# One issue run for each group of two-head products in a hybrid SSD, convolution and attention layer

## The chip, the cores and the metric

One Trainium2 chip, one core. The metric is device time in microseconds (us) of one execution; the median of three runs of the kernel before is 1844.33 us (1840.27 to 1845.91).

## The reference

One layer over 2048 tokens of width 1024. One input projection feeds three mixers, whose gated outputs go through one output projection, a residual and a gated side input. Two of the mixers matter here.

- SSD: 16 heads of 64 columns, chunks of 128 tokens. Per chunk and head, `y = y_diag + y_off`: `y_diag` is a masked 128x128 matrix (made from B, C and the cumulated decays) times the weighted inputs, `y_off` is the decayed C times the state that came into the chunk. The state of a chunk is `h * exp(dec) + new`, one chunk after the other.
- Sliding-window attention: 8 heads of 64, blocks of 128 queries against the block before (kk = 0) and their own block (kk = 1). Softmax weights times values gives the output: two products per block and head, summed.

All is in float32; the projections are made of three products of split halves (high and low part).

## The kernel before, in words

The tokens go in 4 chunks `c` of 512, each of 4 blocks `b` of 128. The first half of the program runs chunks 0 and 1, the second chunks 2 and 3. In each half, units run in the order C0 A0 S0 S1 C1 A1 S2 S3 G1 C2 A2 S4 S5 C3 A3 S6 S7 (line 986): C is convolution, A a pair of attention heads, S a pair of SSD heads, G a group's B and C. Each unit runs for both chunks. A unit has a front (input projections by `proj`, lines 443 to 445, 128x512 products on TensorE, and the eviction of their results) and a back, a Python generator that is put on a list and advanced by one step after every few products of the fronts that follow (`advance`, lines 215 to 218). So the small products of a back are written in between the long products of later fronts.

The framework then fixes the order on every engine when the program is built: a list scheduler with a cost model of its own gives each engine the next instruction whose inputs are made by its reckoning. On the chip every queue runs in that order, and an instruction that waits holds all behind it.

In SSD (`ssd_back`, lines 877 to 944) the back makes `xd` and `xw` (weighted inputs), `eA` and `Ab` (exponentials, from a load of `Ab`, line 868, whose slot in a ring of four 128x1024 tiles, shared with `eA` and with the attention scores, must have come free), four products into `ps_m` (line 910), then the states `H` one after the other on VectorE (line 918, two half-width instructions for each), and then for each block the diagonal products (line 937, `Ab` and `xd`) and the state products (line 940, `eA` and `hin[b]`). Each product has 64 output columns: the two heads of a pair go to partitions 0 to 63 and 64 to 127 of the one `ps_y` bank. The result is read by line 942 and stored by line 944.

In attention (`attn_back`, lines 740 to 861) the weights are transposed on TensorE and copied to `pT` (`turn`, lines 809 to 823), and `mix` (line 838) makes the products with the values, again with two heads in the two halves of `ps_y`. `mix(0)` is written ahead of `turn(1)`, `mix(1)` a step after it.

There are 32 groups of SSD products (8 pairs of heads, 4 chunks) and 16 groups of attention products (4 pairs, 4 chunks). A float32 product shows as two instructions in the trace, so a full group has 32.

Of the kernel before, what the change touches and what calls it, by code (L numbers as in the profile page):

```python
# [14 lines left out]
P = 128  # L15
# [3 lines left out]
TC = 512  # L19
NCHUNK = T // TC  # L20
NB = TC // P
# [40 lines left out]
def hybrid_block_kernel(  # L62
# [16 lines left out]
    V, A, G, PE = nc.vector, nc.scalar, nc.gpsimd, nc.tensor  # L79
# [8 lines left out]
    def ps(tag):  # L88
        return psum.tile([P, TC], F32, tag=tag, name=f"ps_{tag}", bufs=PSB[tag])
# [4 lines left out]
    def t512(name, dtype=F32):  # L94
        return wk.tile([P, TC], dtype, tag="t", name=name, bufs=10)

    def t1024(name):
        return wk.tile([P, 2 * TC], F32, tag="t4", name=name, bufs=4)
# [23 lines left out]
    def pc(name, i=0, n=1):  # L122
        o, w = _par[name]
        return par_sb[:, o + i:o + i + n]
# [221 lines left out]
    with ExitStack() as c1:  # L346
# [10 lines left out]
        hn, rows, kT, vN = {}, {}, {}, {}  # L357
# [144 lines left out]
        def transposes(src):  # L502
            pt = ps("m")
            for b in range(NB):
                PE.transpose(pt[:, b * P:(b + 1) * P], src[:, b * P:(b + 1) * P], ident)
            return pt
# [201 lines left out]
        def attn_front(j, p, c, bias, wq, wg):  # L708
            (pq,) = yield from proj([wq], c)
            qh, ql = t512("qh", F32R), t512("ql", F32R)  # L710
            A.mul(qh, pq, 0.125)
            V.scalar_tensor_tensor(out=ql, in0=pq, scalar=0.125, in1=qh.bitcast(F32), op0=ALU.mult, op1=ALU.subtract)


            qq = [qpair("qh2"), qpair("ql2")]
            for o_ in range(2):
                r = slice(64 * o_, 64 * o_ + 64)
                for t, src in zip(qq, (qh, ql)):
                    for hh in range(2):
                        nc.scalar.dma_start(out=t[r, hh, :].bitcast(F32), in_=src[64 * hh:64 * hh + 64, :].bitcast(F32))  # L720
            yield
            (pg,) = yield from proj([wg], c)
            g2 = silu2(pg, "ag2")
            pending.append(attn_back(j, c, bias, qq, g2))
            yield

        def prev(c, i):

            if c % 2 == 0:
                return kv_tail[i]  # L730
            t = kT[c - 1][i] if i < 2 else vN[c - 1]
            return t[:, TC - P:TC]
# [7 lines left out]
        def attn_back(j, c, bias, qq, g2):  # L740
# [66 lines left out]
            pTs = {}  # L807

            def turn(u):
                for bb in range(2):  # L810
                    b = 2 * u + bb
                    first = c == 0 and b == 0
                    pt = ps("m")
                    for hh in range(2):
                        for kk in range(1 if first else 0, 2):
                            PE.transpose(pt[:, (hh * 2 + kk) * P:(hh * 2 + kk + 1) * P], S[u][:, bb, hh, kk * P:(kk + 1) * P], ident)  # L816
                    pTs[b] = t512("pT")
                    if first:
                        for hh in range(2):
                            s_ = slice((hh * 2 + 1) * P, (hh * 2 + 2) * P)  # L820
                            A.copy(pTs[b][:, s_], pt[:, s_])
                    else:
                        A.copy(pTs[b], pt)

            def mix(u, po):
                for bb in range(2):
                    b = 2 * u + bb
                    first = c == 0 and b == 0
                    for kk in range(1 if first else 0, 2):
                        for hh in range(2):  # L830
                            r = slice(64 * hh, 64 * hh + 64)
                            if kk == 1:
                                vv = vN[c][:, b * P + 64 * hh:b * P + 64 * hh + 64]
                            elif b > 0:
                                vv = vN[c][:, (b - 1) * P + 64 * hh:(b - 1) * P + 64 * hh + 64]
                            else:
                                vv = prev(c, 2)[:, 64 * hh:64 * hh + 64]
                            PE.matmul(  # L838
                                po[r, b * P:(b + 1) * P],
                                lhsT=vv,  # L840
                                rhs=pTs[b][:, (hh * 2 + kk) * P:(hh * 2 + kk + 1) * P],
                                start=(kk == 0 or first),
                                stop=(kk == 1),
                            )

            yield
            scores(0)
# [4 lines left out]
            yield  # L852
            turn(0)
            yield
            po = ps("y")
            mix(0, po)
            turn(1)
            yield
            mix(1, po)
            V.tensor_tensor(out=g2, in0=po, in1=g2, op=ALU.mult)  # L860
            nc.sync.dma_start(out=y_d[12 + j, :, c * TC:(c + 1) * TC], in_=g2)

# [14 lines left out]
        def ssd_back(q, p, c, Ab, xv, z2, tiles, tabs):  # L877
            Bn, CT, CBm = tiles
            dt, acs, eat, dec = tabs
            h0 = 2 * q  # L880
            sl = slice(p * TC, (p + 1) * TC)

            def v4(t):
                return t.rearrange("p (b h d) -> p b h d", b=NB, h=2)

            def bc(t):
                return t[:, p * NB:(p + 1) * NB, h0:h0 + 2].unsqueeze(3).to_broadcast([P, NB, 2, 64])

            def h2(t):
                return t.rearrange("p (h l) -> p h l", h=2)  # L890

            pt = transposes(xv)
            xd = t512("xd")
            V.tensor_tensor(out=v4(xd), in0=v4(pt), in1=bc(dt), op=ALU.mult)
            xw = t512("xw")
            V.tensor_tensor(out=v4(xw), in0=v4(xd), in1=bc(dec), op=ALU.mult)

            eA = t1024("eA")
            A.activation(eA, Ab, AF.Exp)
            for hh in range(2):  # L900
                for b in range(NB):
                    o_ = hh * TC + b * P
                    A.activation(Ab[:, o_:o_ + P], Ab[:, o_:o_ + P], AF.Relu, scale=-1.0, bias=acs[:, p * NB + b, h0 + hh:h0 + hh + 1])  # L903
            A.activation(Ab, Ab, AF.Exp, scale=-1.0)
            yield

            pst = ps("m")
            for b in range(NB):
                bs = slice(b * P, (b + 1) * P)
                PE.matmul(pst[:, bs], lhsT=Bn[:, p * TC + b * P:p * TC + (b + 1) * P], rhs=xw[:, bs], start=True, stop=True)  # L910
            H = tp.tile([P, NB - 1, P], F32, tag="H", name="H", bufs=1)
            hin = [hcar[:, q, :]] + [H[:, b, :] for b in range(NB - 1)]

            def state(b):
                nxt = hin[b + 1] if b < NB - 1 else hcar[:, q, :]
                for hh in range(2):
                    d_ = slice(64 * hh, 64 * hh + 64)
                    V.scalar_tensor_tensor(
                        out=nxt[:, d_],
                        in0=hin[b][:, d_],  # L920
                        scalar=eat[:, p * NB + b, h0 + hh:h0 + hh + 1],
                        in1=pst[:, b * P + 64 * hh:b * P + 64 * hh + 64],
                        op0=ALU.mult,
                        op1=ALU.add,
                    )

            V.tensor_tensor(out=h2(eA), in0=h2(eA), in1=CT[:, sl].unsqueeze(1).to_broadcast([P, 2, TC]), op=ALU.mult)
            V.tensor_tensor(out=h2(Ab), in0=h2(Ab), in1=CBm[:, sl].unsqueeze(1).to_broadcast([P, 2, TC]), op=ALU.mult)
            for b in range(NB - 1):
                state(b)  # L930
            yield
            py = ps("y")
            for b in range(NB):
                bs = slice(b * P, (b + 1) * P)
                for hh in range(2):
                    r = slice(64 * hh, 64 * hh + 64)
                    PE.matmul(py[r, bs], lhsT=xd[:, b * P + 64 * hh:b * P + 64 * hh + 64], rhs=Ab[:, hh * TC + b * P:hh * TC + (b + 1) * P], start=True, stop=False)  # L937
                for hh in range(2):
                    r = slice(64 * hh, 64 * hh + 64)
                    PE.matmul(py[r, bs], lhsT=hin[b][:, 64 * hh:64 * hh + 64], rhs=eA[:, hh * TC + b * P:hh * TC + (b + 1) * P], start=False, stop=True)  # L940
            state(NB - 1)
            V.scalar_tensor_tensor(out=xv, in0=xv, scalar=pc("sd", q), in1=py, op0=ALU.mult, op1=ALU.add)
            V.tensor_tensor(out=xv, in0=xv, in1=z2, op=ALU.mult)
            nc.sync.dma_start(out=y_d[q, :, c * TC:(c + 1) * TC], in_=xv)
# [80 lines left out]
    with ExitStack() as c2:  # L1025
# [4 lines left out]
        for c in range(NCHUNK):  # L1030
# [7 lines left out]
            for n, (dp, kg) in enumerate(steps):  # L1038
# [4 lines left out]
                for kk in range(4):  # L1043
                    yh, yl = ys[4 * kg + kk]
                    first, last = kg + kk == 0, kg == 3 and kk == 3
# [159 lines left out]
```

## Time and profile before

| what | value |
|---|---|
| median of three runs | 1844.33 us |
| the profiled execution | 1850.51 us, of it 1848.7 us span |
| TensorE busy | 1810.7 us (98%) |
| VectorE busy | 1385.1 us (75%) |
| ScalarE busy | 818.6 us (44%) |
| mean granted TensorE clock | 0.994 |

TensorE instructions overlap, and the busy time counts an instruction from its start to its modelled end. What a piece of work costs on TensorE is therefore read here from start to start: from the start of the last instruction ahead of it to the start of the first behind it.

### The profile page before, as it was taken

How to read it: one execution, taken by the hardware profiler on the slowest of the kernel's cores; microseconds unless marked ns; L12 is line 12 of the kernel's file. 1: busy time of each engine (PE TensorE's matmuls, PEld its weight loads, DVE VectorE, ACT ScalarE, POOL GpSimd, SP SyncE). 2: the span in 40 equal slices, each digit the busy share in tenths (PEclk: the TensorE clock that was granted, in tenths of full speed). 3: DMA queues.
4: the chain of work that ended last, by engine and by line, in shares of the span. 5: the costliest groups of instructions: out<-in, count | busy, mean ns of one | idle time of the engine just before them, and what ended most of it. 6: DMA issues, size and time to landing. Idle time of an engine off the chain costs nothing.

```text
span 1848.7 us, 25168 instructions
## 1 busy us (share of the span) xinstructions
PE 1810.7 (98%) x9386; PEld 1461.6 (79%) x9386; DVE 1385.1 (75%) x2400; ACT 818.6 (44%) x1565; POOL 0.2 (0%) x4
## 2 busy tenths in 40 slices
PE   6999999999999999999999999999999999999998
PEld 5877787787888778878788887877888788887887
DVE  6859769759869875976975996988777867466543
ACT  5525425524726542542653371465444444343331
POOL 0000000000000000000000000000000000000000
PEclk9999999999999999999999999999999999999999
DMA  7443233224433433333332332346677766578554
GB/s 234 132 133 98 80 102 96 61 78 106 171 112 111 121 102 104 91 87 89 100 115 76 101 99 87 82 145 230 214 242 236 245 228 199 202 240 280 189 188 131
DMA packets 118982, 265.09 MB, mean 143 GB/s; under 512 B 12619, under 2 KB 20428, under 8 KB 118860
## 3 DMA queue, kind: packets, MB, share of 16 engines
q1 hardware_dynamic: 108428, 246.65, 40.9%
q10 hardware_dynamic: 10432, 16.83, 4.1%
q8 instruction: 74, 1.21, 0.3%
q14 instruction: 48, 0.39, 0.1%
HBM read 205.05 MB, written 39.50 MB: 132 GB/s over the span
## 4 chain that ended last, share of the span: by engine, by line
PE 78%; DMA 8%; DVE 6%; ACT 4%; issue 2%; ACTq 1%; SPq 0%; DVEq 0%
PE ps_pp L443 15%; PE ps_pp L444 14%; PE ps_pp L445 14%; PE ps_pp L1048 4%; PE ps_pp L1049 4%; PE ps_pp L1050 4%; PE ps_pp L208 3%; PE ps_pp L209 3%; PE ps_pp L207 3%; PE ps_m L766 2%; PE ps_y L940 2%; PE ps_y L838 2%; DMA Ab<-acs_d 2%; PE ps_y L937 2%; PE ps_m L816 1%
## 5 line engine op out<-in xcount | busy, mean ns | idle before, releaser
L443 PE MATMUL ps_pp<-al,whi 128*128 128x512 f32 x1344 | 536.6, 400 | 13.6 <-DVE al L393 10.4
L444 PE MATMUL ps_pp<-ah,wlo 128*128 128x512 f32 x1344 | 534.5, 398 | 0.0
L445 PE MATMUL ps_pp<-ah,whi 128*128 128x512 f32 x1344 | 534.1, 397 | 0.0
L191 DVE TENSOR_TENSOR wlo<-wst,whi 128x1024 fp32r<-128x1024 f32 x214 | 234.1, 1102 | 179.8 <-ACT whi L190 179.4
L443 PEld LDWEIGHTS ps_pp<-al,whi 128*128 128x128 f32 x1344 | 254.4, 189 | 73.1 <-DVE al L393 10.4
L190 ACT CAST whi<-wst 128x1024 fp32r<-128x1024 f32 x214 | 202.9, 951 | 242.0 <-DMA wst<-in_w_gate_dram 86.1
L691 DVE SCALAR_TENSOR_TENSOR acc<-gl,par_sb,acc 128x1024 f32<-128x1024 f32 x240 | 307.3, 1280 | 2.3
L444 PEld LDWEIGHTS ps_pp<-ah,wlo 128*128 128x128 f32 x1344 | 254.6, 189 | 55.8 <-issue 6.5
L445 PEld LDWEIGHTS ps_pp<-ah,whi 128*128 128x128 f32 x1344 | 254.5, 189 | 54.4 <-issue 4.9
L489 DVE SCALAR_TENSOR_TENSOR cv<-raw,par_sb,cv 128x512 f32<-128x512 f32 x144 | 107.6, 747 | 22.7 <-ACT cv L487 22.0
L208 PE MATMUL ps_pp<-ah,wlo 128*128 128x512 f32 x256 | 100.2, 391 | 3.7 <-DVE wlo L191 3.7
L1048 PE MATMUL ps_pp<-bl,whi 128*128 128x512 f32 x256 | 101.5, 399 | 0.6 <-ACT whi L190 0.6
L1048 PE MATMUL ps_pp<-al,whi 128*128 128x512 f32 x256 | 100.4, 393 | 0.7 <-DVE al L191 0.7
L1049 PE MATMUL ps_pp<-bh,wlo 128*128 128x512 f32 x256 | 101.1, 395 | 0.0
L1050 PE MATMUL ps_pp<-bh,whi 128*128 128x512 f32 x256 | 100.7, 394 | 0.0
L207 PE MATMUL ps_pp<-al,whi 128*128 128x512 f32 x256 | 100.1, 391 | 0.6 <-ACT whi L190 0.5
L1049 PE MATMUL ps_pp<-ah,wlo 128*128 128x512 f32 x256 | 100.1, 391 | 0.0
L1050 PE MATMUL ps_pp<-ah,whi 128*128 128x512 f32 x256 | 100.0, 390 | 0.0
L209 PE MATMUL ps_pp<-ah,whi 128*128 128x512 f32 x256 | 99.7, 389 | 0.0
L796 ACT ACTIVATE S<-S,nm 128x256 f32<-128x256 f32 (+1 forms) x128 | 62.8, 492 | 80.0 <-DVE nm L782 74.6
L903 ACT ACTIVATE Ab<-Ab,acs 128x128 f32<-128x128 f32 x256 | 82.4, 391 | 0.4
L937 PE MATMUL ps_y<-Ab,xd 128*64 128x128 f32 x512 | 61.5, 282 | 2.0 <-issue 2.0
(235 smaller groups left out, 2592.1 us busy)
## 6 DMA issues: line engine op xcount, KB each, us to landing
wst<-in_w_in_dram SPq DMA_DIRECT2D x88, 512.0 KB, 3.5
wst<-in_w_out_dram SPq DMA_DIRECT2D x64, 512.0 KB, 5.1
Ab<-acs_d SPq DMA_DIRECT2D x64, 256.0 KB, 4.5
ysd<-y_d SPq DMA_DIRECT2D x32, 512.0 KB, 5.5
wst<-in_w_gate_dram SPq DMA_DIRECT2D x32, 512.0 KB, 3.5
gl<-in_xT_dram SPq DMA_DIRECT2D x16, 512.0 KB, 4.0
qh<-qh ACTq DMA_DIRECT2D x64, 128.0 KB, 2.4
ql<-ql ACTq DMA_DIRECT2D x64, 128.0 KB, 2.4
```

The lines of the kernel that those rows point to most:

```text
L190: A.copy(hi, src)
L191: V.tensor_tensor(out=lo, in0=src, in1=hi.bitcast(F32), op=ALU.subtract)
L207: PE.matmul(out, lhsT=hi[:, k, :], rhs=al, start=start and k == 0, stop=False)
L208: PE.matmul(out, lhsT=lo[:, k, :], rhs=ah, start=False, stop=False)
L209: PE.matmul(out, lhsT=hi[:, k, :], rhs=ah, start=False, stop=stop and k == nk - 1)
L443: PE.matmul(o_, lhsT=hi[:, k, :], rhs=al, start=k == 0, stop=False)
L444: PE.matmul(o_, lhsT=lo[:, k, :], rhs=ah, start=False, stop=False)
L445: PE.matmul(o_, lhsT=hi[:, k, :], rhs=ah, start=False, stop=k == KD - 1)
L691: V.scalar_tensor_tensor(out=acc, in0=gl[:, k:k + 2 * TC], scalar=pc("ccw", j * 31 + k), in1=acc, op0=ALU.mult, op1=ALU.add)
L1048: PE.matmul(pj[dd], lhsT=hi[:, i, :], rhs=yl, start=first, stop=False)
L1049: PE.matmul(pj[dd], lhsT=lo[:, i, :], rhs=yh, start=False, stop=False)
L1050: PE.matmul(pj[dd], lhsT=hi[:, i, :], rhs=yh, start=False, stop=last)
```

## The change

Both groups are written out in another order. The instruction whose input is made last goes first (the "head"): block 3's state product in SSD, block 3's own-block product in attention. All others of the group are traced inside `tc.issue_after(head.ins)`, which adds an ordering edge, without a semaphore, from the head to each of them: the scheduler may not issue them ahead of the head. Blocks run from 3 down to 0. In SSD the state products now come ahead of the diagonal ones within a block; in attention the own block comes ahead of the block before. The start and stop flags of the sums follow. In attention both `turn` steps now come ahead of all products, and the products stand in the step in which `mix(1)` stood.

```diff
-            def mix(u, po):
-                for bb in range(2):
-                    b = 2 * u + bb
...
+            def mix(po, b, kk, hh):
...
+                    start=(kk == 1),
+                    stop=(kk == 0 or first),
...
             turn(0)
             yield
+            turn(1)
+            yield
+
             po = ps("y")
-            mix(0, po)
-            turn(1)
-            yield
-            mix(1, po)
+            head = mix(po, NB - 1, 1, 0)
+            with tc.issue_after(head.ins):
+                for b in reversed(range(NB)):
+                    for kk in (1, 0):
+                        for hh in range(2):
+                            if (b, kk, hh) != (NB - 1, 1, 0) and not (kk == 0 and c == 0 and b == 0):
+                                mix(po, b, kk, hh)
...
+            def y_off(b, hh):
...
+            def y_diag(b, hh):
...
+            head = y_off(NB - 1, 0)
+            with tc.issue_after(head.ins):
+                for b in reversed(range(NB)):
+                    for hh in range(2):
+                        if (b, hh) != (NB - 1, 0):
+                            y_off(b, hh)
+                    for hh in range(2):
+                        y_diag(b, hh)
             state(NB - 1)
```

## Rows read from the trace of the kernel before

**Rows 1.** The page: the busy time of the engines, and the lines on the chain that ended last, as shares of the span.

```profile
PE 1810.7 (98%) x9386; PEld 1461.6 (79%) x9386; DVE 1385.1 (75%) x2400; ACT 818.6 (44%) x1565; POOL 0.2 (0%) x4
PE ps_pp L443 15%; PE ps_pp L444 14%; PE ps_pp L445 14%; PE ps_pp L1048 4%; PE ps_pp L1049 4%; PE ps_pp L1050 4%; PE ps_pp L208 3%; PE ps_pp L209 3%; PE ps_pp L207 3%; PE ps_m L766 2%; PE ps_y L940 2%; PE ps_y L838 2%; DMA Ab<-acs_d 2%; PE ps_y L937 2%; PE ps_m L816 1%
```

**Rows 2.** The windows view, three stretches: window, its length in us, then busy us (and instructions) of TensorE, weight loads, VectorE, ScalarE and GpSimd, granted clock, DMA share, GB/s. The first is the units S0 and S1 (four SSD groups), the second has no two-head products, the third is an attention unit.

```profile
184.00:226.00 42.00, 42.00 (x283) 32.18 (x280) 35.00 (x71) 21.90 (x48) 0.00 (x0) 1.00 0.27 87
226.00:282.00 56.00, 55.98 (x258) 46.08 (x256) 38.31 (x59) 14.60 (x34) 0.00 (x0) 1.00 0.32 90
282.00:314.00 32.00, 31.99 (x202) 25.25 (x201) 31.10 (x66) 18.97 (x51) 0.00 (x0) 1.00 0.35 107
```

**Rows 3.** The groups of TensorE instructions by line and shape, those of the two-head products: count, busy us, mean ns of one, idle time before them.

```profile
L937 PE MATMUL ps_y<-Ab,xd 128*64 128x128 f32 x512 | 61.5, 282 | 2.0 <-issue 2.0
L940 PE MATMUL ps_y<-eA,H 128*64 128x128 f32 x384 | 45.6, 280 | 3.6 <-DVE H L918 3.5
L838 PE MATMUL ps_y<-pT,vN 128*64 128x128 f32 x480 | 36.1, 282 | 0.1
...
L940 PE MATMUL ps_y<-eA,hcar 128*64 128x128 f32 x128 | 14.2, 274 | 0.0
...
L838 PE MATMUL ps_y<-pT,tail 128*64 128x128 f32 x16 | 1.8, 298 | 0.0
```

**Rows 4.** The timeline of TensorE, start us and us, for the first SSD group, which issues in three pieces.

```profile
185.42 0.39 PE L445 MATMUL ps_pp<-ah,whi 128*128 128x512 f32 x1
185.73 0.44 PE L937 MATMUL ps_y<-Ab,xd 128*64 128x128 f32 x4
...
186.53 1.16 PE L910 MATMUL ps_m<-xw,Bn 128*128 128x128 f32 x8
187.62 0.43 PE L937 MATMUL ps_y<-Ab,xd 128*64 128x128 f32 x2
187.98 0.50 PE L443 MATMUL ps_pp<-al,whi 128*128 128x512 f32 x1
188.32 0.39 PE L444 MATMUL ps_pp<-ah,wlo 128*128 128x512 f32 x1
...
189.02 0.39 PE L444 MATMUL ps_pp<-ah,wlo 128*128 128x512 f32 x1
189.33 0.44 PE L940 MATMUL ps_y<-eA,H 128*64 128x128 f32 x4
...
190.57 0.50 PE L445 MATMUL ps_pp<-ah,whi 128*128 128x512 f32 x1
```

**Rows 5.** The same view of an SSD group whose 32 instructions already issue in one piece.

```profile
474.87 0.39 PE L443 MATMUL ps_pp<-al,whi 128*128 128x512 f32 x1
475.19 0.44 PE L937 MATMUL ps_y<-Ab,xd 128*64 128x128 f32 x4
475.46 0.39 PE L940 MATMUL ps_y<-eA,hcar 128*64 128x128 f32 x4
...
476.77 0.39 PE L940 MATMUL ps_y<-eA,H 128*64 128x128 f32 x4
477.09 0.50 PE L444 MATMUL ps_pp<-ah,wlo 128*128 128x512 f32 x1
```

**Rows 6.** The same view: the first instructions of the first and the last of the 129 unbroken pieces in which the two-head products issue (44 of attention, 85 of SSD).

```profile
152.83 0.44 PE L838 MATMUL ps_y<-pT,vN 128*64 128x128 f32 x4
...
1253.77 0.44 PE L937 MATMUL ps_y<-Ab,xd 128*64 128x128 f32 x4
```

**Rows 7.** The timeline of VectorE: the first three states of the first SSD group (two halves each).

```profile
187.73 0.47 DVE L918 SCALAR_TENSOR_TENSOR H<-hcar,eat,ps_m 128x64 f32<-128x64 f32 x2 [0.39 <-PE ps_m L910]
188.12 0.85 DVE L918 SCALAR_TENSOR_TENSOR H<-H,eat,ps_m 128x64 f32<-128x64 f32 x4
```

**Rows 8.** The waits of the whole span: who waited for whom, us in total, times, longest.

```profile
ACT eA L899 <- DMA Ab<-acs_d: 44.5, 17, 4.3
...
PE ps_y L940 <- DVE H L918: 3.5, 6, 1.2
...
PE ps_y L937 <- issue: 2.0, 1, 2.0
```

**Rows 9.** The chain that ended last, in the second half's first stretch of SSD units (S0 and S1): start us, us, what.

```profile
793.19 0.33 SPq L868
...
793.57 5.07 DMA Ab<-acs_d
...
798.74 1.07 ACT eA L899
...
799.84 1.86 ACT Ab L903 x6
801.70 0.71 ACT cv L487
...
802.44 0.75 DVE cv L489
803.19 0.20 DVE H L918
...
803.44 0.52 PE ps_y L940 x3
...
804.79 0.32 SPq L868
```

More of the change, by code (lines that the diff above doesn't have):

```diff
@@ L823, in turn @@
                         A.copy(pTs[b], pt)
-            def mix(u, po):
-                for bb in range(2):
-                    b = 2 * u + bb
[L828 to L844, printed above, removed]
+            def mix(po, b, kk, hh):
+                first = c == 0 and b == 0
+                r = slice(64 * hh, 64 * hh + 64)
+                if kk == 1:
+                    vv = vN[c][:, b * P + 64 * hh:b * P + 64 * hh + 64]
+                elif b > 0:
+                    vv = vN[c][:, (b - 1) * P + 64 * hh:(b - 1) * P + 64 * hh + 64]
+                else:
+                    vv = prev(c, 2)[:, 64 * hh:64 * hh + 64]
+                return PE.matmul(
+                    po[r, b * P:(b + 1) * P],
+                    lhsT=vv,
+                    rhs=pTs[b][:, (hh * 2 + kk) * P:(hh * 2 + kk + 1) * P],
+                    start=(kk == 1),
+                    stop=(kk == 0 or first),
+                )
             yield
@@ L854, in attn_back @@
             yield
-            po = ps("y")
-            mix(0, po)
             turn(1)
             yield
-            mix(1, po)
+            po = ps("y")
+            head = mix(po, NB - 1, 1, 0)
[5 more added lines that the diff above has]
+                                mix(po, b, kk, hh)
             V.tensor_tensor(out=g2, in0=po, in1=g2, op=ALU.mult)
@@ L932, in ssd_back @@
             py = ps("y")
[L933 to L940, printed above, removed]
+            def y_off(b, hh):
+                o_ = hh * TC + b * P
+                return PE.matmul(py[64 * hh:64 * hh + 64, b * P:(b + 1) * P], lhsT=hin[b][:, 64 * hh:64 * hh + 64], rhs=eA[:, o_:o_ + P], start=True, stop=False)
+            def y_diag(b, hh):
+                o_, x_ = hh * TC + b * P, b * P + 64 * hh
+                return PE.matmul(py[64 * hh:64 * hh + 64, b * P:(b + 1) * P], lhsT=xd[:, x_:x_ + 64], rhs=Ab[:, o_:o_ + P], start=False, stop=True)
+            head = y_off(NB - 1, 0)
[6 more added lines that the diff above has]
+                        y_diag(b, hh)
             state(NB - 1)
```

## The prediction

> **What bounds the kernel now.** I read the page first: TensorE is busy 98% of the span, VectorE 75%, ScalarE 44%, and most of the chain that ended last is TensorE's [rows 1]. The two-head products stand on that chain with L940, L838 and L937 at 2% each [rows 1], some 110 us, though 1,520 instructions of such a kind [rows 3] need much less, as the next step shows. The windows view says the same of the stages: in a stretch of four SSD groups and in an attention stretch TensorE has no gap; VectorE is at 35.00 of 42 us in the first and at 31.10 of 32 us in the second [rows 2]. So time taken from TensorE's queue is time off the end, as far as the other engines then deliver earlier.
>
> Whether a TensorE that is "busy" throughout has anything to give is the first choice. By its busy time it has none: 42.00 of 42.00 us. The weight loads fill 32.18 of 42 us in the SSD stretch and 46.08 of 56 us in a stretch without two-head products [rows 2]. The Trainium skill (Trainium Kernel Development and Optimization, Performance Expectations) holds that matmul busy time misleads because matmuls are pipelined, and that the share of the weight loads tells more. By that rule the SSD stretch, brought from 77% to the other's 82%, would end 2.9 us sooner, an estimate of 23 us over eight such stretches; by the busy time the sum would be nothing. The start-to-start distances below decide it, and they side with the loads.
>
> **What a piece costs.** The timeline shows the price of going into and out of the 64-column products. The ordinary step from one 512-column product to the next is (189.02 − 188.32) / 3 = 0.23 us [rows 4]. Inside a piece an instruction takes (476.77 − 475.46) / 24 = 0.0546 us [rows 5]. A group in one piece: entry 475.19 − 474.87 = 0.32 us, piece and exit 477.09 − 475.19 = 1.90 us [rows 5], and the first 512-column step behind it 0.34 us (187.98 to 188.32 [rows 4]). Together 2.56 us; less two ordinary steps (0.46) and 32 × 0.0546 (1.75) there remain **0.35 us for entering and leaving once**. A piece that breaks between the two halves of a pair costs 0.10 us more: the piece of two instructions takes 0.36 us with its exit [rows 4], where exit (0.20) and two instructions (0.11) make 0.31, and the piece of ten before it pays likewise.
>
> **What the change removes.** There are 48 groups and 129 pieces [rows 6]. I summed start to start over all 129, less the ordinary steps and less 0.0546 us for each instruction: 59.7 us, of it 16.5 in attention and 43.1 in SSD. About 9 us of that are real waits of TensorE, of which the waits view shows 3.5 us for the states and 2.0 us for `Ab` or `xd` [rows 8], the rest being late entries too short for that view; 1.2 us lie in attention and 8 in SSD. So switching costs 15.3 us in attention and 35.1 in SSD, 0.39 us a piece, which agrees with 0.35 plus the broken pairs. With one piece a group, 16 and 32 times 0.35 are 5.6 and 11.3 us. **The gross gain is 9.7 us in attention and 23.8 us in SSD, 33.5 us.** Numbers of products, loads of weights, DMAs and bytes stay; the flags cost nothing. The 0.35 us per group stays, too.
>
> **What the change adds.** The head may wait, and everything behind it in TensorE's queue, the 512-column products above all, waits with it. In SSD the head needs the third state. The first two halves (first state) span 187.73 to 188.20, and the next four end at 188.97 [rows 7], 0.77 us after the first state; the scheduler can put three or four 512-column products (0.23 us each) into that time, as it put five ahead of the state products in the first group (187.98 to 189.33 [rows 4]), where the third state was 0.36 us early even then. So where VectorE is punctual the head costs nothing; its cover is those products.
>
> Where it is not, the cause is a loop that the chain shows [rows 9]: the end of a group frees a slot, SP issues the load of `Ab` for the group after the next (793.19), it lands 5.07 us later, ScalarE's `eA` has waited for it, six L903 and `cv` follow in its queue, VectorE's `cv`, then the state (803.19), and TensorE, waiting, starts the state products at 803.44. ScalarE waited 44.5 us in 17 such places [rows 8]. Two loads in each stretch of four groups are tied like this, 16 heads in all. SP stands too while it waits for the slot, with weight loads and `y_d` stores behind it. There the state's time does not move with TensorE, so what TensorE has saved in the groups before is waited away. From below this costs nothing (the loads come early enough, or ScalarE's order loosens), from above it takes all 23.8 us. I take half, since two heads in four are tied: 11.9 us lost.
>
> In attention the head waits for the last `pT`, as `mix(1)` did; the first half's products lose their early place, which costs only the time of 16 instructions behind the head, and no TensorE product waits for the result. VectorE is full there (31.10 of 32 us [rows 2]), so part of a faster TensorE will find scores or split weights late: between nothing and the 9.7 us; I take a quarter, 2.4 us, since the stretch between leaves VectorE room to catch up (38.31 of 56 us [rows 2]). `ps_y`, a single bank, is held for a shorter time by both; four `pT` are held a step longer, which no row prices: between nothing and one step of three or four 512-column products a group, 16 × 0.9 = 14 us; I take nothing, because no wait for a slot shows on TensorE.
>
> Sum: 33.5 − 11.9 − 2.4 = 19.2 us. The profiled execution is 1850.5 us (span 1848.7), 6.2 us above the median; it would become 1831.3, and the median 1844.3 − 19.2 = **1825**.
>
> **The rivals.** *All is kept* (0.20): waits stay at their 9 us, 1844.3 − 33.5 = 1811. For it: seven SSD groups go in one piece already, several with no wait [rows 5]; moving the diagonal products behind the head hardly moves the group's end. Against: the tied loads. *SSD keeps nothing* (0.15): every stretch is as long as its loads make it, only 7.3 us of attention remain, 1837. For it: the loop from 793.19 to 804.79 is 11.6 us [rows 9], and TensorE, without a gap, spends 42 / 4 = 10.5 us on a group's share of a stretch [rows 2].
>
> *The head lengthens the loop* (0.08), the rival on the slower side: in a tied group the loop now closes through the third state and the whole run. From the first state to SP's issue it took 803.39 to 804.79, 1.4 us [rows 9]; the third state (0.77 later) and a run of 1.75 plus landing of the last product make 2.7, so 1.3 us more, twice in a stretch, less the four 512-column products that went ahead (0.92): 1.7 us × 8 stretches = 14 us lost on top of the SSD gain, less 7.3 us of attention: 1851. It decides once the 16 tied heads wait 2.0 us more on average than such places do now (33.5 − 2.4 over 16). Against it: the scheduler puts the later `Ab` load later in ScalarE's order as well, so `cv` and the state would come less late than the load.
>
> *No single run* (0.12): the edge forbids the others to come before the head, not other work to come between them; if the scheduler still finds 512-column products to slip in, the pieces stay and the time is 1844 within 4. Against it: behind the last-made input all are ready at once.
>
> **How the numbers follow.** The forecast has 0.45. Differences below 0.3% (5.5 us) can't be told from none here. Faster: forecast, all kept, and SSD keeps nothing, 0.45 + 0.20 + 0.15 = 0.80; same 0.12; slower 0.08. The range runs from 1809, which takes in the gross gain, to 1842, which takes in the loss of all SSD gain and part of the case without change; the slower rival, half of the unchanged case and a few in a hundred below the low end stay out.
>
> **What would show it.** Right: 48 to about 55 pieces instead of 129, TensorE's steps at 0.35 us per group, L940's wait for `H` grown from 3.5 us to some 15 us and placed on the head alone, in the second and third groups of a stretch. The time comes off ahead of the last piece, now at 1253.77 [rows 6], and hardly behind it. Wrong: pieces above 80, or waits of 30 us on the heads, or TensorE waiting for split weights or for a `ps_pp` bank in the attention stretches.

## The result, and the profile after

The changed kernel takes 1832.29 us (median of 7 runs, 1824.26 to 1837.59) against 1844.40 us of the kernel before in the same comparison: ratio 0.9935, 95% interval 0.9917 to 0.9952, **12.1 us faster** where 19.2 were forecast. The profiled execution took 1835.88 us, 14.6 less than the one of before; single executions of one kernel differ by up to some 15 us, so the terms below, read from one profile each, add up only to within that.

The page after, the engines' busy time and its chain, answering to [rows 1]:

```profile
PE 1785.7 (97%) x9386; PEld 1460.3 (80%) x9386; DVE 1383.7 (75%) x2400; ACT 815.3 (44%) x1565; POOL 0.2 (0%) x4
PE ps_pp L443 11%; PE ps_pp L444 11%; PE ps_pp L445 11%; DVE acc L691 4%; PE ps_pp L1060 4%; PE ps_pp L1062 4%; PE ps_pp L1061 4%; DMA Ab<-acs_d 3%; PE ps_pp L208 3%; PE ps_pp L209 3%; PE ps_pp L207 3%; DVE wlo L191 2%; PE ps_y L939 2%; PE ps_m L766 2%; DMA wst<-in_w_gate_dram 1%
```

TensorE does the same 9,386 instructions in 25 us less busy time. Of the two-head products only L939 (the state products, L940 before) is still on the chain's line; `Ab`'s load has gone from 2% to 3%.

The timeline of TensorE in the second half's first SSD group, start us and us, shows the run that answers to [rows 4, 5]: state product of block 3 first, `hcar` last, nothing in between.

```profile
780.57 0.39 PE L444 MATMUL ps_pp<-ah,wlo 128*128 128x512 f32 x1
780.89 0.44 PE L939 MATMUL ps_y<-eA,H 128*64 128x128 f32 x4
781.16 0.39 PE L943 MATMUL ps_y<-Ab,xd 128*64 128x128 f32 x4
...
782.47 0.39 PE L943 MATMUL ps_y<-Ab,xd 128*64 128x128 f32 x4
782.79 0.50 PE L445 MATMUL ps_pp<-ah,whi 128*128 128x512 f32 x1
783.12 0.40 PE L443 MATMUL ps_pp<-al,whi 128*128 128x512 f32 x1
```

Entry 0.32, run and exit 1.90, first step behind it 0.33 us, the numbers of [rows 4, 5]. There are 52 pieces now instead of 129: 16 in attention, 36 in SSD, where four groups still have a break after their first two instructions.

The time comes off where the pieces are, as forecast. The same two 512-column products, the one ahead of the first piece of before and the one behind the last piece of after, start in the profile before and in the one after at:

```profile
152.51 0.39 PE L445 MATMUL ps_pp<-ah,whi 128*128 128x512 f32 x1
1259.88 0.39 PE L1049 MATMUL ps_pp<-ah,wlo 128*128 128x512 f32 x1
...
151.42 0.39 PE L445 MATMUL ps_pp<-ah,whi 128*128 128x512 f32 x1
1244.39 0.50 PE L1061 MATMUL ps_pp<-ah,wlo 128*128 128x512 f32 x1
```

The stretch between them went from 1107.4 to 1093.0 us, 14.4 us less; what lies ahead of it is 1.1 us shorter, what lies behind it 0.9 us longer.

The waits of TensorE after, us in total, times, longest, answering to [rows 8]:

```profile
PE ps_m L912 <- DVE xw L898: 7.0, 5, 2.0
PE ps_y L939 <- DVE H L920: 4.5, 6, 1.3
...
PE ps_y L939 <- ACT Ab L905: 2.4, 3, 1.0
```

The first line is new. L912 makes the chunk states (L910 before) and hardly waited for `xw` before the change. The windows view, columns as in [rows 2], has gaps in TensorE where there were none (184 to 226 us) or small ones (787 to 830 us: 42.20 of 43 us busy before, the first line of the second window). The windows lie at the same times, so that they hold slightly other work:

```profile
184.00:226.00 42.00, 40.48 (x290) 33.38 (x290) 34.40 (x71) 20.08 (x43) 0.00 (x0) 1.00 0.29 89
...
787.00:830.00 43.00, 42.20 (x284) 33.10 (x285) 35.78 (x71) 21.75 (x47) 0.00 (x0) 1.00 0.30 81
787.00:830.00 43.00, 39.96 (x252) 32.76 (x252) 26.60 (x53) 16.54 (x32) 0.00 (x0) 0.96 0.19 62
```

Where the new wait comes from is told by VectorE's timeline and the chain at 782 to 791 us. First VectorE (start, us, and in brackets its idle time and what ended it):

```profile
786.08 0.69 DVE L896 TENSOR_TENSOR xd<-ps_m,dt 128x512 f32<-128x512 f32 x1 [0.38 <-PE ps_m L505]
789.28 1.23 DVE L929 TENSOR_TENSOR eA<-eA,CT 128x1024 f32<-128x1024 f32 x1 [2.51 <-ACT eA L901]
790.42 0.69 DVE L898 TENSOR_TENSOR xw<-xd,dec 128x512 f32<-128x512 f32 x1
```

`xw` (L898) has had its input since 786.77, but stands behind L929, which multiplies the `eA` of the *next* group, and VectorE waits 2.51 us for that. `xw` itself waits for nothing else: VectorE has no idle time just ahead of it. In the stretch of [rows 9], before the change, `xw` stood ahead of the next `eA` product:

```profile
798.99 0.69 DVE L896 TENSOR_TENSOR xw<-xd,dec 128x512 f32<-128x512 f32 x1
799.84 1.23 DVE L927 TENSOR_TENSOR eA<-eA,CT 128x1024 f32<-128x1024 f32 x1 [0.16 <-ACT eA L899]
```

The chain of the stretch after the change says why that `eA` was late:

```profile
782.88 0.15 SPq L870
...
783.09 5.00 DMA Ab<-acs_d
...
788.19 1.07 ACT eA L901
...
790.42 0.70 DVE xw L898
...
791.26 2.04 PE ps_m L912 x8
```

The end of a group's run frees the slot, the load of `Ab` takes 5.00 us, ScalarE makes `eA`, VectorE multiplies it, only then comes `xw`, and TensorE starts L912. It is the loop of [rows 9], closed at another place than the head.

### The profile page after: what moved, and what is told of

The parts are those of the page before. It is cut to its first block, busy times and chain, and to the rows that moved or that the text cites. A ratio compares the mean times of both kernels' runs of the same rounds, so it can differ in the third digit from the quotient of the medians.

```text
span 1834.1 us, 25184 instructions
## 1 busy us (share of the span) xinstructions
PE 1785.7 (97%) x9386; PEld 1460.3 (80%) x9386; DVE 1383.7 (75%) x2400; ACT 815.3 (44%) x1565; POOL 0.2 (0%) x4
## 4 chain that ended last, share of the span: by engine, by line
PE 65%; DVE 14%; DMA 12%; ACT 5%; issue 3%; ACTq 1%; SPq 0%; DVEq 0%
PE ps_pp L443 11%; PE ps_pp L444 11%; PE ps_pp L445 11%; DVE acc L691 4%; PE ps_pp L1060 4%; PE ps_pp L1062 4%; PE ps_pp L1061 4%; DMA Ab<-acs_d 3%; PE ps_pp L208 3%; PE ps_pp L209 3%; PE ps_pp L207 3%; DVE wlo L191 2%; PE ps_y L939 2%; PE ps_m L766 2%; DMA wst<-in_w_gate_dram 1%
## 5 line engine op out<-in xcount | busy, mean ns | idle before, releaser
L444 PEld LDWEIGHTS ps_pp<-ah,wlo 128*128 128x128 f32 x1344 | 254.6, 189 | 51.3 <-issue 1.7
L489 DVE SCALAR_TENSOR_TENSOR cv<-raw,par_sb,cv 128x512 f32<-128x512 f32 x144 | 107.7, 748 | 13.3 <-ACT cv L487 12.1
L905 ACT ACTIVATE Ab<-Ab,acs 128x128 f32<-128x128 f32 x256 | 81.7, 391 | 0.5
L208 PEld LDWEIGHTS ps_pp<-ah,wlo 128*128 128x128 f32 x256 | 48.4, 189 | 15.3 <-DVE wlo L191 5.4
```

Source lines behind the costliest of these rows:

```text
L208: PE.matmul(out, lhsT=lo[:, k, :], rhs=ah, start=False, stop=False)
L444: PE.matmul(o_, lhsT=lo[:, k, :], rhs=ah, start=False, stop=False)
```

## The experiments

Each kernel was timed in five rounds beside the kernel before on the same chip; ratios are to that kernel.

**The two halves of the change.** `attn_only` has the attention part with the SSD products as before, `ssd_only` the reverse.

> Attention part of the change alone, SSD as before: 90 pieces of two-head products instead of 129. Switching theory (a piece costs about 0.39 us, waits small): 28 pieces fewer and 10 to 11 us less, near 1834. Rival A (four pT held longer use up the ring of ten 512-column tiles, so that xw gets a slot that only a store of y_d frees, and stands back in VectorE's queue): the saving is eaten in the SSD units that follow, 1840 to 1844, with waits of L910-like products for xw. Rival B (the loop through the Ab load eats what SSD saves): nothing eaten here, near 1834.

Measured: 1833.65 us, ratio 0.9961 (0.9945 to 0.9977), some 7 us less; TensorE waits 1.3 us, once, for `xw`. The switching theory's size is missed by 3 to 4 us (its time of 1834 is met because the kernel before took 1840.97 us on this chip). Rival A's is missed, too: nothing like all is eaten. The expectation counts the pieces wrongly, besides: from 129 to 90 it is 39 pieces less, 28 of attention and 11 of SSD, whose code is the old one but whose products the scheduler places anew. At 0.39 us each, 39 pieces are 15 us, of which half was kept.

> SSD part of the change alone, attention as before: 82 pieces. Gross saving of the SSD part by the trace 21 to 24 us. Rival A (ring of 512-column tiles, caused by the attention part): nearly all of it is kept, 1823 to 1826, no waits for xw. Rival B (loop through the Ab load): half is eaten, 1832 to 1836, waits on the head or for xw in the second and third group of each stretch.

Measured: 1842.52 us, ratio 1.0004 (0.9985 to 1.0023): **the SSD part alone keeps nothing**, less than either theory left it. Part of that goes with TensorE's clock: the mean granted clock (the share of the full clock that the chip granted) was 0.9943 over these 12 executions and 0.9966 over the 23 of the kernel before. A straight line through the times of the 12 falls by 2.1 us for each 0.001 of the clock (by 1.4 us in the 12 of `before_q5` below), so the lower clock stands for an estimated 3 to 5 us; no trace shows where they fell, for the profiled execution (1836.6 us) is one of the quickest and had 0.998. The pieces of `ssd_only` are 82, and the waits in that profile are these:

```profile
PE ps_m L910 <- DVE xw L896: 10.5, 7, 1.8
PE ps_y L937 <- ACT Ab L903: 3.9, 5, 1.2
...
PE ps_y L937 <- DVE H L918: 1.7, 2, 1.1
```

No `xw` of the second or third group of a stretch waits for a stored tile here, so rival A cannot be the cause; the wait for `xw` is there all the same, and larger than with both parts.

**The order of two instructions.** In the built program the `eA` product stands ahead of the `xw` of the group before in five groups before the change, in eight with `attn_only`, in nine with `ssd_only` and in ten with both parts, four of these ten second in their stretch. TensorE's five waits for `xw` in the changed kernel are at five of the ten, those four among them, and the seven of `ssd_only` at seven of its nine. `xw_first` forbids this order:

```diff
-            V.tensor_tensor(out=v4(xw), in0=v4(xd), in1=bc(dec), op=ALU.mult)
+            xw_prev = last_xw[-1] if last_xw else None
+            last_xw.append(V.tensor_tensor(out=v4(xw), in0=v4(xd), in1=bc(dec), op=ALU.mult))
...
-            V.tensor_tensor(out=h2(eA), in0=h2(eA), in1=CT[:, sl]..., op=ALU.mult)
+            with tc.issue_after(xw_prev.ins) if xw_prev is not None else ExitStack():
+                V.tensor_tensor(out=h2(eA), in0=h2(eA), in1=CT[:, sl]..., op=ALU.mult)
```

> The whole change, and in VectorE's queue the eA product of a group may no longer stand ahead of xw of the group before it (in the changed kernel it does so in ten groups). If the 9 us of waits of the state products' input (L912 for xw) come from that order, behind an eA that waits for the Ab load, they fall to under 2 us and the time is 1822 to 1826. If xw waits for its own slot (ring of 512-column tiles), it waits all the same: 1830 to 1834.

Measured: 1821.34 us, ratio 0.9894 (0.9874 to 0.9915), which just misses the 0.9917 to 0.9952 of the change alone. The waits:

```profile
PE ps_y L942 <- DVE H L922: 4.4, 6, 1.0
...
PE ps_m L914 <- DVE xw L900: 3.2, 1, 3.2
```

Five waits for `xw` became one (of 3.2 us, more than the 2 expected). That one is of the same kind, behind another instruction: `xw` (L900) stands behind L434, which waits for a load of `acc`:

```profile
584.07 0.75 DVE L434 SCALAR_TENSOR_TENSOR gl<-gl,par_sb,acc 128x512 f32<-128x512 f32 x1 [3.27 <-DMA acc<-row]
584.73 0.69 DVE L900 TENSOR_TENSOR xw<-xd,dec 128x512 f32<-128x512 f32 x1
```

The rule moves much else in the built order, so two controls go with it: the rule in the kernel before, and the rule with the SSD part alone.

> Control: the kernel before, with the one rule that the eA product may not stand ahead of xw of the group before in VectorE's queue (it does so in five groups). The kernel before hardly waits for xw (0.35 us in all). If the rule pays only together with the single runs: 122 pieces instead of 129, 1838 to 1841. If the rule is a gain of its own, whatever the pieces are: 1826 to 1832.

Measured: 1837.32 us, ratio 0.9975 (0.9959 to 0.9990): some 4.6 us, near the first case. Not all of the 20 us of `xw_first` belong to the single runs, but only about a quarter comes with the rule alone.

> The SSD part of the change alone, with the same rule. If the order behind the eA that waits for its Ab load is what ate the SSD part: waits of L910-like products for xw fall from 12 us to under 4, and 10 to 15 us come back, 1826 to 1832. If the loop through the Ab load binds by any path (rival B), the wait moves to the heads, which then wait 12 us or more instead of 6: 1836 to 1841.

Measured: 1826.63 us, ratio 0.9924 (0.9908 to 0.9940). The SSD part with the rule gives 14 us, of which the rule alone gave 4.6; without the rule it gives none. Its waits for `xw` are gone, and the heads wait 5.0 us in all, not 12:

```profile
PE ps_y L940 <- DVE H L920: 5.0, 10, 0.7
```

**The ring of 512-column tiles.** `after_t11` is the changed kernel with one buffer more:

```diff
-        return wk.tile([P, TC], dtype, tag="t", name=name, bufs=10)
+        return wk.tile([P, TC], dtype, tag="t", name=name, bufs=11)
```

> The whole change with 11 instead of 10 buffers of 512 columns. The order of VectorE's queue around xw stays that of the changed kernel; only the waits of xw for a stored tile fall from 14 to 6. Rival A (ring): 1822 to 1826. Rival B (order behind the Ab load): 1830 to 1834, waits of L912 for xw still 7 to 9 us.

Measured: 1829.96 us, ratio 0.9932 (0.9910 to 0.9953), the same as the change alone. `xw`'s waits for a stored tile fell from 14 to 6 in the built program and TensorE's wait for `xw` is 6.2 us instead of 7.0. Three of the 6 are second in their stretch, so this run alone would not end rival A; with `ssd_only`, and with no idle time of VectorE ahead of `xw`, it falls.

**The load of `Ab`.** With five 128x1024 buffers the load need not wait for the end of the group before last. The rule of the order is in `xw_q5` and not in `after_q5`; `before_q5` is the control.

```diff
-        return wk.tile([P, 2 * TC], F32, tag="t4", name=name, bufs=4)
+        return wk.tile([P, 2 * TC], F32, tag="t4", name=name, bufs=5)
...
-        v = wk.tile([P, n], F32, tag="rs_v", name="rs_v", bufs=2)
+        v = wk.tile([P, n], F32, tag="rs_v", name="rs_v", bufs=1)
```

(and likewise for `rs_i`, `rs_g` and `rs_t`)

> The whole change with the rule, and five instead of four 128x1024 buffers (64 bytes for it come from single-buffered scratch columns of the reciprocal root): the load of Ab need no longer wait for the end of the group before last. If that loop holds the heads, their waits fall from 6 us to under 2 and ScalarE's waits for Ab from about 40 us to under 10: 1811 to 1816. If the heads wait for VectorE's own queue, 1819 to 1823.

Measured: 1819.21 us, ratio 0.9880 (0.9864 to 0.9896): not told apart from `xw_first` by the intervals. The waits did what the first case of the expectation said, the time what the second said. The heads' waits fell to 0.7 us, once. ScalarE still stands for 38.5 us in front of `eA`, but for the slot of `eA` itself, and no longer for the load:

```profile
ACT eA L903 <- PE ps_y L942: 38.5, 15, 5.2
```

> The whole change with five 128x1024 buffers and without the rule: xw stands behind the eA product of the next group in 16 groups instead of ten, but the Ab load that this eA waits for no longer waits for the end of the group before last. If the cost of that order is the wait for the Ab load, the waits of L912 for xw vanish (under 2 us) and it comes near the version with both, 1817 to 1823. If the order costs by itself (xw late by one eA product of 1.2 us in 16 groups): waits of 8 us or more and 1828 to 1834.

Measured: 1822.62 us, ratio 0.9905 (0.9887 to 0.9922). `xw` stands behind the next `eA` product in 16 groups, more than ever, yet:

```profile
PE ps_y L939 <- DVE H L920: 0.9, 1, 0.9
PE ps_m L912 <- DVE xw L898: 0.7, 1, 0.7
```

So it is not the order by itself that costs, but the order together with a load that comes late. Taking away either takes the waits away; the times of `xw_first` and `after_q5` agree within their intervals, that of `after_q5` touching the interval of the change alone.

> Control: the kernel before with five 128x1024 buffers. If the loop through the Ab load costs the kernel before its 6 us of waits at the state products and at Ab: 1834 to 1837, with ScalarE's waits for Ab under 10 us. If these waits have another cause: 1839 to 1842. It has 124 pieces instead of 129, worth 2 us by itself.

Measured: 1839.98 us, ratio 0.9996 (0.9984 to 1.0008). The kernel before gains nothing from the fifth buffer: its two-head products start late by 1.4 us in all instead of 7.6, and the time is the same. One thing on record goes against it: the mean granted clock was 0.9941 over its 12 executions and 0.9964 over the 23 of the kernel before, an estimated 3 to 5 us by the two lines above. Why the clock is lower no run here shows.

The ordering edge itself needed no run: without `issue_after` the built program is the same on all queues, instruction by instruction. It is the written order, last-made input first, that makes the run.

## Why the prediction was right, and where it was off

- **Pieces and their price: right.** 52 pieces (48 to 55 forecast). Summed start to start as in the prediction, entering and leaving cost 51 us in 129 pieces before and 19.3 us in 52 pieces after, 0.40 and 0.37 us each. The gross gain of 33.5 us measures 31.8: 9.8 in attention, 22.0 in SSD.
- **TensorE's limit: right.** The load share of the first SSD stretch rose from 77% to 33.38 / 42 = 79% with a TensorE that now has gaps, on the way to the other stretch's 82%. The sentence on the load share, drawn from the Trainium skill (Trainium Kernel Development and Optimization, Performance Expectations), thus agrees in direction: a TensorE that was busy 42.00 of 42.00 us had time to give.
- **Attention: right in the number; the loss is not shown to be the one forecast.** A quarter of 9.7 us was to be lost, and `attn_only` keeps some 7 us, as forecast (7.3). But `attn_only` also lost 11 pieces of SSD, worth some 4 us, so that about half of its gain was lost, not a quarter, and that the sum came out so near is luck to that extent. No run shows that the loss lies in late scores or split weights; a lower mean granted clock (0.9952 against 0.9966) may be 2 to 3 us of it. The four `pT` held longer cost nothing that can be measured (`after_t11`).
- **The loss in SSD: right in where it starts, the late load of `Ab`, wrong in its path.** The step "the head may wait" expected the heads' waits to grow to some 15 us, and that sign did not come: summed with late entries they were 7.6 us before and are 7.6 us after. The wait fell on L912 instead: the term priced TensorE's queue, but the group's new end also moved the scheduler's order on VectorE, which put a product that waits for the late load ahead of the `xw` that the same group needs. Outside the two-head products, late starts of TensorE grew from 7.6 to 23.2 us between 150 and 1258 us of the span, 9.2 us of the latter at L912. That is 15.6 us lost beside 31.8 gained, 16 us net by these accounts (14.4 in the stretch between the two 512-column products named at the start, 14.6 in the span, 12.1 in the medians). The forecast lost 14.3. Its 11.9 us for SSD were half of a range from nothing to all, taken for waits that did not grow; that another loss came near that size is luck.
- **Half is kept in SSD: not confirmed.** Alone, the SSD part keeps nothing (1.0004), as the rival "SSD keeps nothing" had it; with the attention part the ratios 0.9935 and 0.9961 leave it some 5 us, and their intervals overlap. That rival's 1837 and the forecast's 1825 lie on either side of 1832, and the rival's is the nearer. Its reason, that every stretch is as long as its loads make it, falls all the same: `xw_first` has the same four buffers and the same loads and takes 1821.34 us.
- **The lengthened loop: fell.** The heads did not wait 2 us more, and the time is not longer. **No single run: fell.**
- **The scheduler's looser order, argued against the loop: came in part.** At the place of [rows 9] `cv` stands in ScalarE's queue behind four L905 where six L903 stood, and starts 2.3 us after `eA` (788.19 to 790.47) instead of 3.0 (798.74 to 801.70 [rows 9]). What that is worth no run shows; the rule of `xw_first` is on VectorE's order.

By the same accounts `xw_q5` saves 35 us on TensorE (31.5 of switching, 6.8 of late heads, less 3 of other late starts), but its ratio is worth only 22 us. The profiles agree with the accounts: the stretch between the two 512-column products named at the start takes 1072.4 us there (153.49 to 1225.90) instead of 1107.4, and the span 1817.4 us instead of 1848.7. What the ratio lacks lies in the other executions: the profiled one of the kernel before (1850.51 us) is 10 us longer than that kernel's median beside `xw_q5` (1840.24), and the mean granted clock of `xw_q5` is 0.9940 against 0.9964, an estimated 3 to 5 us. What stays open is why kernels with the fifth buffer, and `ssd_only`, run at a lower mean clock than the kernel before (`after_q5` 0.9928 against 0.9971), and so what the fifth buffer would be worth at an equal one.

## What to carry to other kernels

Count the pieces in which products of another array shape issue, not only their busy time; 0.4 us for each entry and exit is invisible in an engine that is "98% busy". After a change of order on one engine, look at what a list scheduler did with the queues of the others, first of all at instructions that wait for a transfer and have short work of an earlier group behind them. Where a gain is eaten, ask for both ends of the wait: pinning the order of two VectorE instructions, or giving the load one buffer more, brought back 5 to 8 us. And set the granted clocks side by side before a difference in time is read as one in work.

## What the runs showed of the hardware that was not expected

In the changed kernel TensorE stood for 1.99 us ahead of L912 at 791.26 us and then had a granted clock of half the full one for some 3.4 us. The timeline of TensorE there:

```profile
788.88 0.39 PE L445 MATMUL ps_pp<-ah,whi 128*128 128x512 f32 x1
791.26 2.04 PE L912 MATMUL ps_m<-xw,Bn 128*128 128x128 f32 x8 [1.99 <-DVE xw L898]
792.95 0.77 PE L443 MATMUL ps_pp<-al,whi 128*128 128x512 f32 x1
793.52 0.63 PE L444 MATMUL ps_pp<-ah,wlo 128*128 128x512 f32 x1
793.95 0.63 PE L445 MATMUL ps_pp<-ah,whi 128*128 128x512 f32 x1
794.38 0.54 PE L443 MATMUL ps_pp<-al,whi 128*128 128x512 f32 x1
794.75 0.40 PE L444 MATMUL ps_pp<-ah,wlo 128*128 128x512 f32 x1
```

The steps between 512-column products are 0.43 us instead of 0.23, which is the lower level of 1.2 GHz; the windows of 4 us show a granted clock of 0.57 there and of 1.00 behind the wait of 1.62 us at 922.11:

```profile
791.00:795.00 4.00, 3.74 (x14) 3.39 (x15) 3.28 (x10) 2.49 (x6) 0.00 (x0) 0.57 0.00 0
922.00:926.00 4.00, 3.89 (x31) 3.25 (x33) 3.81 (x10) 2.81 (x7) 0.00 (x0) 1.00 0.00 0
```

From 791.26 to 794.75 the eight products and four steps took 3.49 us; at the full level, in the same profile, eight such products took 0.81 us (803.72 to 804.53) and the step behind them 0.31, which with three steps of 0.23 makes 1.8 us. So a wait of 2 us cost 1.7 us more behind it.

Nor does the clock fall behind waits alone. In `xw_q5` it was half from 104.5 to 118.1 us, though TensorE had been busy for 8.50 of the 8.50 us ahead, with the weight loads busy for 4.10 of them:

```profile
96.00:104.50 8.50, 8.50 (x27) 4.10 (x26) 2.60 (x7) 3.66 (x7) 0.00 (x0) 1.00 0.44 142
104.50:118.10 13.60, 13.60 (x25) 6.66 (x24) 1.76 (x4) 4.15 (x9) 0.00 (x0) 0.50 0.31 105
```
